# Opening of a two-layer encoder: raw x in its own tiles, two small loads on another queue, and fourteen matmuls on zeros

## The chip, the cores and the metric

One core of a Trainium2 chip runs the whole program; the other cores are idle. The metric is the device time of one execution in microseconds (us), the median of several runs. Profiles come from the hardware profiler; times in them count from the start of the span, that is from the first instruction that the profiler saw on the core. Engines are PE (TensorE), DVE (VectorE), ACT (ScalarE), POOL (GpSimd) and SP, which here only issues transfers; SPq and ACTq are the sequencers of SP and ACT, which issue them.

## What is computed

The reference is a residual trunk of two layers over 256 tokens of width 2048, in float32, with a final norm:

```python
def reference(x, norm_g, final_g, w_in_even, w_out_even, rpb_b, w_in_odd, w_out_odd, sinks_c, qnorm_d, knorm_d):
    h = x
    for layer in range(DEPTH):                     # DEPTH = 2
        y = rms_norm(h, norm_g[layer])
        if layer % 2 == 0:
            h = h + even_layer(y, w_in_even[0], w_out_even[0], rpb_b[0])
        else:
            h = h + odd_layer(y, w_in_odd[0], w_out_odd[0], sinks_c[0], qnorm_d[0], knorm_d[0])
    return rms_norm(h, final_g)
```

Each layer projects y with one wide matrix, runs two kinds of attention on the parts of the result, multiplies each by a gate and projects back. Only the first projection of the even layer matters here: `y @ w_in_even` for the first 512 columns of values ("v"), a product of 256 tokens by 2048 by 512.

## The kernel before, in words

The kernel works in float32 accuracy with a faster matmul type: each operand is cut into a high part (`hi`, rounded to that type) and a low part (`lo`, the rest), and a product is three matmuls, hi by hi, hi by lo, lo by hi (`mm3`, L100). The norm's per-token factor is applied after the projection, so the projection starts from raw x, scaled only by the norm's gain per feature (`gcol`).

Weights stream through. `plan` (L76, filled at L509 to L524) lists all weight blocks in the order of use, each 128 partitions x 1024 float32 (512 KB). `weights()` (L78) keeps two blocks ahead: a `Weights` object (L52) takes a raw buffer (`wraw`, pool `wp` with **five** buffers), loads it on SP's queue, makes `hi` on ACT (L69) and `lo` on DVE (L70), each with three buffers. A raw buffer is free again when both have read it.

The opening is the first `by_token` (L260): eight blocks j = 0 to 7 of the values' weights, called w0 to w7 below, each with the two 128-feature slices of x that multiply it (x0 to x7, 256 KB each, held transposed in DRAM as `xt`). These eight `Weights` objects also load x into `xraw`, **a second buffer of the same pool of five** (L61 to L67), and scale and cut it: `hi` by ACT (L95), `lo` by DVE (L96), the function `split`. For j = 0 both loads are cut in two halves (w0a, x0a, w0b, x0b), so that the first matmuls can start early. All these loads are `pinned` (L85): they go out in the order of the program on SP. For each j there are 12 matmuls of 512 columns (two slices, two halves of the tokens, three products each), 96 in all. Beside them `opening` (L528) issues the loads of the first two of four parts of h (x again, by token; h0 at j = 6, h1 at j = 7); the other two follow after the opening (L561).

After the opening come three projections `by_feature` (L241; q, k, gate), with four weight blocks each (the first is f0), and then attention beside further projections. A list of generators (`evac`, `bg`) is advanced by `step()` after each block: it holds `first_scale` (L535), which squares and sums h on ACT (L184) and makes the norm's factor, and then the evictions of the accumulators. The engines' instruction order is made by the framework from the program's order and the dependencies; only pinned instructions keep the program's order among themselves.

The tiles `mh0` to `mh7` (128 x 2 x 256 each) hold the results of the eight attentions of each layer; the first of them is written only when the first attention has ended. `pth` holds transposed probabilities of attention, and the PSUM tile `o` its output.

Of the kernel before, what the change touches and what calls it, by code (L numbers as in the profile page):

```python
# [9 lines left out]
F32 = mybir.dt.float32  # L10
F32R = mybir.dt.float32r
BF16 = mybir.dt.bfloat16
I32 = mybir.dt.int32
AF = mybir.ActivationFunctionType
ALU = mybir.AluOpType
AX = mybir.AxisListType

P = 128
D = 2048
S = 256  # L20
HD = 128
KC = D // P
KK = 2
NJ = KC // KK
# [3 lines left out]
BIG = 1e30  # L28
GRID_W = 64
AHEAD = 2  # L30
RPB_R, RPB_C = 15, 31


@with_exitstack
def encoder(ctx, tc, a, out):
    nc = tc.nc
    pool = lambda name, bufs, **kw: ctx.enter_context(tc.tile_pool(name=name, bufs=bufs, **kw))
    const = pool("const", 1)
    big = pool("big", 1)
    wp = pool("wp", 5)  # L40
    hp = pool("hp", 3)
    pp = pool("pp", 2)
    tp = pool("tp", 2)
# [5 lines left out]
    ps_o = pool("ps_o", 1, space=PS)  # L49


    class Weights:  # L52


        def __init__(self, src, hi=None, lo=None, x=None):
            raw = wp.tile([P, 1024], F32, tag="wraw", name="wraw")
            self.hi = hi or hp.tile([P, 1024], F32R, tag="whi", name="whi")
            self.lo = lo or hp.tile([P, 1024], F32R, tag="wlo", name="wlo")
            cuts = KK if x == 0 else 1
            cols = [slice(i * 1024 // cuts, (i + 1) * 1024 // cuts) for i in range(cuts)]  # L60
            xraw = [wp.tile([P, KK, S], F32, tag="wraw", name="xraw")] if x is not None else []  # L61
            for i, c in enumerate(cols):
                load = nc.sync.dma_start if x is None else pinned
                load(raw[:, c], src[:, c])
                for r in xraw:
                    k = slice(i, i + 1) if cuts > 1 else slice(0, KK)
                    pinned(r[:, k], a["xt"][x].rearrange("p (k t) -> p k t", k=KK)[:, k])  # L67
            for i, c in enumerate(cols):
                nc.scalar.copy(self.hi[:, c], raw[:, c])  # L69
                nc.vector.tensor_sub(self.lo[:, c], raw[:, c], self.hi[:, c].bitcast(F32))  # L70
                for r in xraw:
                    for m in (i,) if cuts > 1 else range(KK):
                        k = x * KK + m
                        split(xh[k], xl[k], r[:, m, :], gcol[:, k : k + 1])

    plan, ready = [], []  # L76

    def weights(ahead=AHEAD):  # L78

        while plan and len(ready) <= ahead:  # L80
            src, x = plan.pop(0)
            ready.append(Weights(src, x=x))
        return ready.pop(0)

    def pinned(dst, src):  # L85

        tc.keep_in_program_order(nc.sync.dma_start(dst, src))

    def split(hi, lo, src, scale=None):

        if scale is None:
            nc.scalar.copy(hi, src)
            nc.vector.tensor_sub(lo, src, hi.bitcast(F32))
        else:
            nc.scalar.mul(hi, src, scale)  # L95
            nc.vector.scalar_tensor_tensor(  # L96
                out=lo, in0=src, scalar=scale, in1=hi.bitcast(F32), op0=ALU.mult, op1=ALU.subtract
            )
# [10 lines left out]
    xh = [X[k // 4][:, k % 4, 0, :] for k in range(KC)]  # L109
    xl = [X[k // 4][:, k % 4, 1, :] for k in range(KC)]  # L110
    h = [big.tile([P, 2, 512], F32, tag=f"h{n}", name=f"h{n}") for n in range(NN)]

    gcol = const.tile([P, 2 * KC], F32, tag="gcol", name="gcol")
    nc.scalar.dma_start(gcol, a["norm_g"])
    warm = const.tile([P, 1], F32, tag="warm", name="warm")
    nc.vector.memset(warm, 0.0)
    nc.scalar.activation(warm, warm, AF.Exp)
# [10 lines left out]
    def load_h(n):  # L128
        x = a["x"].rearrange("(t p) d -> p t d", p=P)
        pinned(h[n], x[:, :, n * 512 : (n + 1) * 512])  # L130
# [17 lines left out]
    def rsqrt(dst, ss, n, mean):  # L148

        x = sm.tile([P, n], F32, tag="rs_x", name="rs_x")  # L150
        nc.vector.tensor_scalar(x, ss, mean, EPS, ALU.mult, ALU.add)
        y = sm.tile([P, n], I32, tag="rs_y", name="rs_y")
        nc.vector.tensor_scalar(y, x.bitcast(I32), -0.5, 1597463007.0, ALU.mult, ALU.add)
        y = y.bitcast(F32)
        for it in range(3):
            t = sm.tile([P, n], F32, tag="rs_t", name="rs_t")
            nc.vector.tensor_mul(t, y, y)
            nc.vector.scalar_tensor_tensor(t, t, -0.5, x, ALU.mult, ALU.mult)
            z = dst if it == 2 else sm.tile([P, n], F32, tag="rs_z", name="rs_z")
            nc.vector.scalar_tensor_tensor(z, t, 1.5, y, ALU.add, ALU.mult)  # L160
            y = z
# [18 lines left out]
    def square_sums(parts, n, t=None):  # L180

        for tt in range(2) if t is None else (t,):
            junk = tp.tile([P, 512], BF16, tag="junk", name="junk", bufs=1)
            nc.scalar.activation(junk, h[n][:, tt, :], AF.Square, accum_out=parts[:, tt, n : n + 1])  # L184

    def row_scale(layer, parts):

        ss = sm.tile([P, 2], F32, tag="ss", name="ss")
        nc.vector.tensor_reduce(ss, parts, AX.X, ALU.add)
        r = const.tile([P, 2], F32, tag=f"rstd{layer}", name=f"rstd{layer}")  # L190
        rsqrt(r, ss, 2, 1.0 / D)
        return r

    def spread_scale(r):

        bc = ps_at.tile([P, S], F32, tag="at", name="ps_bc")
        for tt in range(2):
            t = tp.tile([P, P], F32, tag="rb", name="rb")
            nc.vector.tensor_scalar_mul(t, ones, r[:, tt : tt + 1])
            nc.tensor.transpose(bc[:, tt * P : (tt + 1) * P], t, ident)  # L200
        rk = const.tile([P, S], F32, tag="rk", name="rk")
        rq = const.tile([P, S], F32, tag="rq", name="rq")
        nc.vector.tensor_copy(rk, bc)
        nc.vector.tensor_scalar_mul(rq, rk, -SCALE)
        rhalf = const.tile([P, S], F32, tag="rhalf", name="rhalf")
        nc.vector.tensor_scalar_mul(rhalf, rk, 0.5)
        return rk, rq, rhalf
# [151 lines left out]
    mh = [big.tile([P, 2, S], F32R, tag=f"mh{i}", name=f"mh{i}") for i in range(8)]  # L359
# [168 lines left out]
    def opening(j):  # L528
        if j == 2:
            make_identity(nc, ident)  # L530
            nc.gpsimd.memset(ones, 1.0)
        if j > 5:
            load_h(j - 6)

    def first_scale():  # L535
        yield
        yield
        for n in range(NN):
            square_sums(parts0, n)
        r = row_scale(0, parts0)  # L540
        yield
        scales[0] = r, spread_scale(r)
        yield
# [26 lines left out]
    for u in range(4):  # L570
        st = {}
        if u == 1:
            bg.append(later_consts())
        for pr, kind in even_order(u):
            if kind != "v":
                evac.append(evict_even(2 * u + pr, kind, by_feature(), st))
                continue
            if u:
                acc = by_token(512, token_acc())
            else:  # L580
                acc = [ps_at.tile([P, 512], F32, tag="at", name="ps_t") for _ in range(2)]
                by_token(512, acc, opening)
                bg.append(after_opening())
                evac.append(first_scale())
            st["v"] = values_tile()
            evac.append(evict_even(2 * u, kind, acc, st))
# [13 lines left out]
    def tail_even(order):  # L600
        for n in range(NN):
            accs = out_accs()
            project_out(order, accs)
            for t in range(2):
                add_h(n, t, accs[t])
            for c in range(2):
                tr = ps_at.tile([P, 2, S], F32, tag="at", name="ps_ht")
                for i in range(2):
                    for t in range(2):
                        nc.tensor.transpose(  # L610
                            tr[:, i, t * P : (t + 1) * P],
                            h[n][:, t, (2 * c + i) * P : (2 * c + i + 1) * P], ident,
                        )
                for i in range(2):
                    k = 4 * n + 2 * c + i
                    split(xh[k], xl[k], tr[:, i, :], gcol[:, KC + k : KC + k + 1])
            square_sums(parts1, n)
# [209 lines left out]
```

## Time and profile before

| | |
|---|---|
| median of 3 runs | 839.94 us (839.72 to 842.06) |
| the profiled execution | 839.72 us |
| its span, first to last instruction | 837.6 us |
| PE busy | 821.5 us, 98% of the span, 4472 matmuls |
| DVE, ACT, POOL busy | 67%, 53%, 2% |
| moved by DMA | 158.51 MB, mean 189 GB/s |
| opening: first matmul, first matmul of the next projection | 4.80 us, 30.58 us |

The profiled execution is the quickest of the three runs shown, 0.22 us below the median, and 2.1 us of it lie outside the span. A matmul's duration in the trace reaches into the next one's, since they are pipelined; the rate of the engine is read from the distance between starts.

### The profile page before, as it was taken

The numbers are of one execution on the slowest core, as the hardware profiler recorded it, in microseconds if no ns is written. First come the engines' busy times: TensorE is split into PE (matmuls) and PEld (weight loads), VectorE is DVE, ScalarE is ACT, GpSimd is POOL, SyncE is SP. The second block draws the span as 40 slices with busy tenths as digits, with TensorE's granted clock in tenths as the row PEclk, the third lists the DMA queues.
The fourth block names the chain that finished last, engine by engine and source line by source line (L and its number), as shares of the span: only waits on it lengthen the run. The fifth ranks groups of instructions, "written<-read, shape, count | busy, mean of one in ns | idle before, by whom it ended". The sixth has DMA issues, their size and how long they took to land.

```text
span 837.6 us, 11876 instructions
## 1 busy us (share of the span) xinstructions
PE 821.5 (98%) x4472; PEld 707.2 (84%) x4472; DVE 559.5 (67%) x873; ACT 445.1 (53%) x706; POOL 18.8 (2%) x24
## 2 busy tenths in 40 slices
PE   7999999999999999999999999999999999999995
PEld 5888888888888888888888888888899888888884
DVE  5677575667757675576645787786976666766547
ACT  6755454555445554455443565556666555664433
POOL 0000000000001010010000000000000000000000
PEclk9999999999999999999999999999999999999998
DMA  7976765655566565665555555654545555655622
GB/s 253 374 228 204 236 208 170 209 176 175 178 199 194 171 199 168 201 196 160 172 184 192 176 175 180 193 184 150 165 162 191 182 179 188 194 191 193 226 90 100
DMA packets 55577, 158.51 MB, mean 189 GB/s; under 512 B 14112, under 2 KB 15008, under 8 KB 55456
## 3 DMA queue, kind: packets, MB, share of 16 engines
q1 hardware_dynamic: 55376, 157.74, 57.7%
q8 instruction: 35, 0.57, 0.3%
q14 instruction: 22, 0.18, 0.1%
q10 hardware_dynamic: 144, 0.02, 0.0%
HBM read 155.64 MB, written 3.05 MB: 189 GB/s over the span
## 4 chain that ended last, share of the span: by engine, by line
PE 97%; DVE 1%; DMA 1%; ACT 0%; SPq 0%; issue 0%; DVEq 0%; ACTq 0%
PE ps_f L250 33%; PE ps_f L254 16%; PE ps_t L103 13%; PE ps_t L104 13%; PE ps_t L102 13%; PE ps_pt L439 2%; PE ps_s L103 1%; PE ps_s L104 1%; PE ps_out L103 1%; PE ps_out L104 1%; PE ps_s L102 1%; PE ps_out L102 1%; DMA wraw<-in_even_t 1%; PE ps_ht L610 0%; DVE h L495 0%; PE ps_tr L352 0%
## 5 line engine op out<-in xcount | busy, mean ns | idle before, releaser
L70 DVE TENSOR_TENSOR wlo<-wraw,whi 128x1024 fp32r<-128x1024 f32 (+1 forms) x269 | 329.5, 1225 | 209.7 <-ACT whi L69 208.6
L69 ACT CAST whi<-wraw 128x1024 fp32r<-128x1024 f32 (+1 forms) x269 | 281.8, 1048 | 345.5 <-PE ps_t L104 146.9
L250 PE MATMUL ps_f<-x,whi 128*128 128x512 f32 x1184 | 374.0, 397 | 0.0
L254 PEld LDWEIGHTS ps_f<-x,wlo 128*128 128x128 f32 x1184 | 222.3, 188 | 53.0 <-DVE wlo L70 0.7
L254 PE MATMUL ps_f<-x,wlo 128*128 128x256 f32 x1184 | 233.4, 278 | 0.0
L250 PEld LDWEIGHTS ps_f<-x,whi 128*128 128x128 f32 x1184 | 180.9, 189 | 0.4
L102 PE MATMUL ps_t<-whi,x 128*128 128x512 f32 (+1 forms) x256 | 97.7, 382 | 5.6 <-ACT x L95 5.6
L103 PE MATMUL ps_t<-wlo,x 128*128 128x512 f32 (+1 forms) x256 | 97.2, 380 | 0.3 <-DVE wlo L70 0.3
L104 PE MATMUL ps_t<-whi,x 128*128 128x512 f32 (+1 forms) x256 | 97.2, 380 | 0.0
L102 PE MATMUL ps_t<-whi,mh 128*128 128x512 f32 x240 | 94.1, 392 | 0.0
L103 PE MATMUL ps_t<-wlo,mh 128*128 128x512 f32 x240 | 94.0, 391 | 0.0
L104 PE MATMUL ps_t<-whi,ml 128*128 128x512 f32 x240 | 93.6, 390 | 0.0
L102 PEld LDWEIGHTS ps_t<-whi,x 128*128 128x128 f32 x256 | 48.4, 189 | 14.9 <-ACT x L95 6.8
L104 PEld LDWEIGHTS ps_t<-whi,x 128*128 128x128 f32 x256 | 48.4, 189 | 9.7 <-DVE x L96 0.6
L103 PEld LDWEIGHTS ps_t<-wlo,x 128*128 128x128 f32 x256 | 48.5, 189 | 9.2 <-DVE wlo L70 1.0
L104 PEld LDWEIGHTS ps_t<-whi,ml 128*128 128x128 f32 x240 | 45.1, 188 | 9.2
L103 PEld LDWEIGHTS ps_t<-wlo,mh 128*128 128x128 f32 x240 | 45.2, 188 | 8.9
L102 PEld LDWEIGHTS ps_t<-whi,mh 128*128 128x128 f32 x240 | 45.1, 188 | 8.9
L469 DVE TENSOR_TENSOR mx<-ps_out,silu 128x512 f32<-128x512 f32 x16 | 11.1, 691 | 30.1 <-PE ps_out L104 30.1
L495 DVE TENSOR_TENSOR h<-ps_t,h 128x512 f32<-128x512 f32 x32 | 21.1, 685 | 9.7 <-PE ps_t L104 9.5
L421 ACT ACTIVATE pr<-lg,mn 128x256 f32<-128x256 f32 (+1 forms) x48 | 23.9, 500 | 5.0 <-DVE mn L409 5.0
L294 DVE TENSOR_TENSOR qf<-ps_f,qf 128x512 f32<-128x512 f32 x37 | 25.2, 682 | 0.0
(116 smaller groups left out, 657.0 us busy)
## 6 DMA issues: line engine op xcount, KB each, us to landing
wraw<-in_even_f SPq DMA_DIRECT2D x96, 512.0 KB, 3.5
wraw<-in_odd_f SPq DMA_DIRECT2D x56, 512.0 KB, 3.4
wraw<-in_w_out_even SPq DMA_DIRECT2D x32, 512.0 KB, 3.3
wraw<-in_w_out_odd SPq DMA_DIRECT2D x32, 512.0 KB, 4.2
wraw<-in_even_t SPq DMA_DIRECT2D x31, 512.0 KB, 4.2
wraw<-in_odd_t SPq DMA_DIRECT2D x24, 512.0 KB, 3.6
h<-in_x SPq DMA_DIRECT2D x4, 512.0 KB, 8.0
bias<-in_bias_a SPq DMA_DIRECT2D x8, 256.0 KB, 5.2
```

What stands on the lines that cost most here:

```text
L69: nc.scalar.copy(self.hi[:, c], raw[:, c])
L70: nc.vector.tensor_sub(self.lo[:, c], raw[:, c], self.hi[:, c].bitcast(F32))
L102: nc.tensor.matmul(dst, lh, rh, start=first, stop=False, skip_group_check=True)
L103: nc.tensor.matmul(dst, lh, rl, start=False, stop=False, skip_group_check=True)
L104: nc.tensor.matmul(dst, ll, rh, start=False, stop=last, skip_group_check=True)
L250: nc.tensor.matmul(acc[:, f, :], w.hi[:, c], xx[k], start=k == 0, stop=False, skip_group_check=True)
L254: nc.tensor.matmul(acc[:, f, :S], w.lo[:, c], xh[k], start=False, stop=k == KC - 1, skip_group_check=True)
L294: nc.vector.tensor_add(f, acc[:, :, :S], f)
L421: nc.scalar.activation(p[:, t, :W], lg[:, t, :W], AF.Exp, bias=mn[:, t : t + 1], scale=-1.0, accum_out=den[:, t : t + 1],)
L439: nc.tensor.transpose(tr[:, c, t * P : (t + 1) * P], p[:, t, c * P : (c + 1) * P], ident)
L469: nc.vector.tensor_mul(m, o, silu)
L495: nc.vector.tensor_add(h[n][:, t, :], acc, h[n][:, t, :])
```

## The change

Five edits, all around the opening:

- Raw x no longer takes buffers of the weights' pool. Eight tiles with the names `mh0` to `mh7` hold it (`xraw[j]`), the same memory that later holds the results of attention. So the five raw buffers are for weights alone.
- The two halves of x0 are issued on ACT's queue, behind the load of `gcol` and ahead of ACT's table load; SP now begins with w0a, w0b, w1, x1, w2, x2.
- For j = 0 the high part of x is made on DVE instead of ACT, and ahead of the cut of the weights in program order.
- A tile of zeros is set on DVE (128 x 256, in the memory of `pth`), and 14 matmuls of it by itself (256 columns each) go into the PSUM tile `o`, ahead of all else on PE.
- h0 and h1 are loaded at j = 4 and j = 6 instead of 6 and 7; the squares on ACT are pinned; `first_scale` yields after h1 and h3, so it takes two steps more.

```diff
+WARM = 14
...
-            xraw = [wp.tile([P, KK, S], F32, tag="wraw", name="xraw")] if x is not None else []
-            for i, c in enumerate(cols):
+            for c in cols:
                 load = nc.sync.dma_start if x is None else pinned
                 load(raw[:, c], src[:, c])
-                for r in xraw:
-                    k = slice(i, i + 1) if cuts > 1 else slice(0, KK)
-                    pinned(r[:, k], a["xt"][x].rearrange("p (k t) -> p k t", k=KK)[:, k])
+            if x:
+                load_xraw(x, slice(0, KK), nc.sync)
             for i, c in enumerate(cols):
+                if x == 0:
+                    nc.vector.tensor_scalar_mul(xh[i], xraw[0][:, i, :], gcol[:, i : i + 1])
                 nc.scalar.copy(self.hi[:, c], raw[:, c])
                 nc.vector.tensor_sub(self.lo[:, c], raw[:, c], self.hi[:, c].bitcast(F32))
-                for r in xraw:
-                    for m in (i,) if cuts > 1 else range(KK):
-                        k = x * KK + m
-                        split(xh[k], xl[k], r[:, m, :], gcol[:, k : k + 1])
+                if x == 0:
+                    low_x(i)
+            if x:
+                for k in range(x * KK, (x + 1) * KK):
+                    split(xh[k], xl[k], xraw[x][:, k % KK, :], gcol[:, k : k + 1])
+
+    def load_xraw(j, k, engine):
+        src = a["xt"][j].rearrange("p (k t) -> p k t", k=KK)
+        tc.keep_in_program_order(engine.dma_start(xraw[j][:, k], src[:, k]))
+
+    def low_x(k):
+        nc.vector.scalar_tensor_tensor(
+            out=xl[k], in0=xraw[k // KK][:, k % KK, :], scalar=gcol[:, k : k + 1], in1=xh[k].bitcast(F32),
+            op0=ALU.mult, op1=ALU.subtract,
+        )
...
     nc.scalar.dma_start(gcol, a["norm_g"])
+    xraw = [big.tile([P, KK, S], F32, tag=f"mh{j}", name="xraw") for j in range(NJ)]
+    load_xraw(0, slice(0, 1), nc.scalar)
+    load_xraw(0, slice(1, 2), nc.scalar)
+    idle = tp.tile([P, S], F32R, tag="pth", name="idle")
+    nc.vector.memset(idle.bitcast(F32), 0.0)
+    ps_idle = ps_o.tile([P, S], F32, tag="o", name="ps_idle")
+    for _ in range(WARM):
+        nc.tensor.matmul(ps_idle, idle[:, :P], idle, start=True, stop=True, skip_group_check=True)
...
-            nc.scalar.activation(junk, h[n][:, tt, :], AF.Square, accum_out=parts[:, tt, n : n + 1])
+            tc.keep_in_program_order(
+                nc.scalar.activation(junk, h[n][:, tt, :], AF.Square, accum_out=parts[:, tt, n : n + 1])
+            )
...
-        if j > 5:
-            load_h(j - 6)
+        if j in (4, 6):
+            load_h(j // 2 - 2)
...
         for n in range(NN):
             square_sums(parts0, n)
+            if n % 2:
+                yield
```

## Rows read from the trace of the kernel before

**Rows 1.** Profile page, part 4: the chain that ended last, by engine

```profile
PE 97%; DVE 1%; DMA 1%; ACT 0%; SPq 0%; issue 0%; DVEq 0%; ACTq 0%
```

**Rows 2.** Chain of waits in order of time, 0 to 13 us: start, duration, what

```profile
2.57 6.18 DMA wraw<-in_even_t
...
8.78 1.06 ACT whi L69
...
9.86 1.24 DVE wlo L70
...
11.14 0.50 PE ps_t L103
```

**Rows 3.** Timeline of PE: start, duration, line, out<-in, size, count [idle before]

```profile
4.80 0.80 PE L102 MATMUL ps_t<-whi,x 128*128 128x512 f32 x1 [4.80 <-ACT x L95]
...
6.68 0.63 PE L103 MATMUL ps_t<-wlo,x 128*128 128x512 f32 x1
7.10 0.63 PE L104 MATMUL ps_t<-whi,x 128*128 128x512 f32 x1
...
10.28 0.51 PE L102 MATMUL ps_t<-whi,x 128*128 128x512 f32 x1 [0.51 <-ACT x L95]
...
19.49 0.39 PE L103 MATMUL ps_t<-wlo,x 128*128 128x512 f32 x1
...
20.11 0.40 PE L102 MATMUL ps_t<-whi,x 128*128 128x512 f32 x1
...
27.87 0.41 PE L103 MATMUL ps_t<-wlo,x 128*128 128x512 f32 x1
...
28.52 0.39 PE L102 MATMUL ps_t<-whi,x 128*128 128x512 f32 x1
...
30.58 0.61 PE L250 MATMUL ps_f<-x,whi 128*128 128x512 f32 x2
...
31.57 0.63 PE L250 MATMUL ps_f<-x,whi 128*128 128x512 f32 x2
```

**Rows 4.** Timeline of SP: the issues of w0b, w1, x2, h0 and f0

```profile
1.62 0.43 SPq L87 DMA_DIRECT2D wraw<-in_even_t  x1
...
2.57 0.43 SPq L87 DMA_DIRECT2D wraw<-in_even_t  x1
...
7.05 0.33 SPq L87 DMA_DIRECT2D xraw<-in_xt  x1
...
21.66 0.43 SPq L87 DMA_DIRECT2D h<-in_x  x1
22.18 0.42 SPq L64 DMA_DIRECT2D wraw<-in_even_f  x1
```

**Rows 5.** Windows of the opening: busy time by engine, clock, DMA share, GB/s

```profile
1.00:4.00 3.00, 0.00 (x0) 0.00 (x0) 0.00 (x0) 1.76 (x3) 0.36 (x2) 1.00 0.67 198
4.00:6.00 2.00, 1.20 (x3) 1.04 (x4) 1.09 (x2) 1.07 (x3) 0.00 (x0) 1.00 0.50 158
6.00:9.00 3.00, 2.67 (x9) 1.50 (x8) 1.17 (x2) 1.03 (x3) 0.00 (x0) 1.00 0.99 376
```

**Rows 6.** Timeline of ACT, 0 to 8 us

```profile
1.15 1.28 ACT L117 ACT_TABLE_LOAD   x1 [1.15 <-PEq L817]
...
3.72 0.62 ACT L69 CAST whi<-wraw 128x512 fp32r<-128x512 f32 x1 [1.08 <-DMA wraw<-in_even_t]
...
7.50 0.51 ACT L95 ACTIVATE x<-xraw,gcol 128x256 fp32r<-128x256 f32 x1 [1.21 <-DMA xraw<-in_xt]
```

**Rows 7.** Timeline of DVE: first release of a projection's accumulator, and a scaling

```profile
43.23 0.68 DVE L294 TENSOR_TENSOR qf<-ps_f,qf 128x512 f32<-128x512 f32 x1
...
46.34 0.28 DVE L204 TENSOR_SCALAR rq<-rk 128x256 f32<-128x256 f32 x1
```

**Rows 8.** Windows after the last matmul (columns as in Rows 5)

```profile
826.00:828.00 2.00, 1.56 (x7) 0.94 (x6) 1.89 (x8) 1.37 (x5) 0.00 (x0) 1.00 0.00 0
...
830.00:832.00 2.00, 0.00 (x0) 0.00 (x0) 1.77 (x7) 0.10 (x1) 0.00 (x0) 0.59 0.78 289
```

## The prediction, on record before the changed kernel was built

> **What bounds the kernel now.** I read the chain that ended last first: 97% of it is PE [rows 1]. From the middle of the opening to the end PE is one unbroken stream, so nothing that speeds another engine there matters; what the change can give is only the time by which this stream starts earlier. The second view, the chain in order of time [rows 2], shows what starts it: the load of w1, issued at 2.57, lands at 8.75; ACT makes its high part from 8.78, DVE its low part from 9.86 to 11.10, and at 11.14 PE goes on and hardly stops again. The third view, PE's timeline [rows 3], shows what lies before and behind this point. The first matmul is at 4.80. Early ones are 0.42 us apart (6.68 to 7.10), which is 512 columns at 1.2 GHz; later ones 0.228 us (34 steps from 20.11 to 27.87), which is 2.4 GHz. At 11.14 only 13 of 96 matmuls have run. The other 83 would take 83 x 0.228 = 18.92 us and end at 30.06; they end at 30.58. So 0.52 us are lost behind 11.14: two steps from 19.49 take 0.62 instead of 0.46, and two from 27.87 take 0.65. Four matmuls from 30.58 (two of 512 columns, two of 256, so 3 x 0.228 = 0.68) take 0.99: 0.31 lost. Together 0.83 us.
>
> Last, the transfers. SP has issued w1 by 3.0 [rows 4], but x2 goes out only at 7.05: it waits for a buffer of the five. The windows [rows 5] show that the transfer engines are not full: 594 KB by 4.0 (3 us at 198 GB/s), then a share of 0.50 and 158 GB/s from 4 to 6 although w1 is queued, then 0.99 and 376 GB/s.
>
> **The change part by part.** The reference is the profiled execution: 839.72 us, 0.22 under the median.
>
> *Zeros on PE.* Fourteen matmuls of 256 columns. No row shows one at half clock; by columns each is half of 0.42, so 14 x 0.21 = 2.9 us. They start when DVE has set the tile, about 1.2 (a set of this size should not exceed the 0.28 us of a scaling of 128 x 256 [rows 7], from about 0.8), and end at 4.2, before the first real matmul can run. Bounds: 14 x 0.114 = 1.6 us at full clock, and 14 x 0.42 = 5.9 us if each costs as much as one of 512 columns, which ends at 7.1. I take 2.9, as the cost goes by columns at 2.4 GHz too. Their use is the clock: before, the spacing shows the rise between 7.10 and 8.1, some 3.2 us after the first matmul. Started at 1.2, PE should have 2.4 GHz at about 4.4 to 5. That spares the 12 matmuls of j = 0 six times 0.2 us = 1.2 us. But this stretch lies ahead of the wait for w1: the next matmul is at 10.28 after idling [rows 3]. So I put it at nothing. The Trainium skill, in "TensorE: Matmul & The Clock Gate", section on the HAM clock gate, says that half rate is the default which activity lifts, and advises to warm up; by that page the sum would gain the 1.2 us, and by the rows none, for what PE saves there it waits.
>
> *First matmul.* DVE makes the high part of x0a beside ACT's cast, not behind it. ACT casts w0a from 3.72 [rows 6]; a scaling costs 0.28 on DVE [rows 7]. The first matmul moves from 4.80 to about 4.45. This too ends in the wait for w1: nothing. ACT issues two loads more before its table load at 1.15: two issues of 0.43 [rows 4] put the table's end from 2.43 to about 3.4, still ahead of 3.72; without that cover it delays w0a, not w1.
>
> *Order of the loads, the term that decides.* On SP, w1 goes out behind w0a and w0b alone, 1.62 instead of 2.57 [rows 4]: 0.95 earlier. The x0 halves come by ACT's queue at the same time. How much earlier does w1 land? Lower bound: nothing, if the 1311 KB up to the end of w1 pass in the same order at the same pace. Upper bound: engines full from 4.0. Then 1311 - 594 = 717 KB at 376 GB/s end at 5.9; before, that much had moved by about 7.2 (4.0 to 6.0 brought 316 KB, the other 401 KB took 1.1 us or more), while the landing came at 8.75, 1.55 us behind, as the slowest of the engines counts. 5.9 + 1.55 = 7.45, a gain of 1.3. I take 0.95, the earlier issue passed on in full, since the share of 0.50 says that transfer engines lacked work while w1 had long been issued; it is nearer to the upper bound for that reason. The wait chain behind is unchanged: landing 7.8, high part 7.83 to 8.9, low part to 10.15, stream from 10.2. The 12 matmuls of j = 0 must be done by 9.3, when w1's first x is cut: from 4.45 they need 2.7, and x0b, which landed at 7.5 [rows 6], is issued half a microsecond sooner. They are.
>
> *Buffers for weights alone.* w3 and w4 no longer wait for a buffer; x2 (before at 7.05) and what follows are issued by 5. All that PE uses after w1 lands well ahead of it. I take 0.65 of the 0.83 us of later stalls as gone, with bounds of nothing (if ACT's and DVE's own order is what is late) and 0.83.
>
> *h loads and squares.* h0 stands ahead of w6 now instead of ahead of f0 [rows 4], one load of 512 KB, 1.4 us at 376 GB/s, with several us of lead by then: nothing; without that lead, up to 1.4 us. SP waits longest for a raw buffer of w5 onward, and behind that wait stand x5 and h0, all with lead. The eight squares remain on ACT, one pair of steps later. What depends on them is the norm's factor; q's accumulator is released by a DVE addition at 43.23 that does not use it [rows 7], and the third projection needs that bank at 30.58 + 2 x (32 x 0.228 + 32 x 0.114) = 52.5. Two steps of 2.7 us later fit in: nothing; without the cover PE would stand up to 3 us there.
>
> **Sum.** 0.95 + 0.65 = 1.6 us: 839.72 - 1.6 = 838.1 for an execution like the profiled one, 838.3 as a median.
>
> **Rivals.**
>
> (a) *The supply does not move.* The two queues feed the same 16 transfer engines, w1 still lands at 8.75, and only the later stalls go: 839.94 - 0.65 = 839.3. For it: from 6 to 9 the share is 0.99, and the slowest engine decides. Against it: the half-empty stretch at 4 to 6. The Trainium skill, "DMA: Bandwidth & Descriptors", section "Issuing engines are not separate DMA queues", says that loads started from several engines interleave on the same engines and save only the issuer's time; the 0.50 of the trace says there was room, and which of them holds decides between (a) and the forecast.
>
> (b) *The supply moves more.* The hole at 4 to 6 closes and the spread between the transfer engines shrinks, so that w1 lands at 6.5 or before: 2.25 + 0.65 = 2.9 us, 837.0. The limit is a stream from 4.45: opening over at 4.45 + 96 x 0.228 = 26.3, a gain of 4.2 + 0.3 = 4.5, or 835.4. For it: no other work keeps PE then. Against it: even with full transfer engines, the sum above comes to 7.45.
>
> (c) *Slower.* PE, now early, is done with j = 0 at 7.4 and then idles until w1. If w1 lands as late as before, that is until 10.28, 2.9 us. At the end of the run the clock shows what idling does: last of seven matmuls over at 827.6, mean clock 0.59 in 830 to 832, so it fell at 830.4, 2.8 us after [rows 8]. From an idle time of that length the clock falls, and the stream begins at half rate: over the 3.2 us until it rises, 1.6 us are lost. 839.94 - 0.65 + 1.6 = 840.9. Against it: it wants a late w1 and a quick j = 0 together.
>
> **How the numbers follow.** Forecast 0.50, (a) 0.24, (b) 0.18, (c) 0.08. About 0.3%, 2.5 us, is what a measurement of this kernel can tell from no change. Faster by that needs 837.4 or less: (b), 0.18. Slower needs 842.5, which (c) reaches only together with a late release of q's bank: 0.04. Same: 0.78. The range reaches from inside (b), 836.5, to between (a) and (c), 840.3; the forecast's own bounds are 837.8 to 839.9.
>
> **What would show it.** Right: first matmul near 4.45, spacing 0.228 from about 5 on, w1's cast at about 7.8, unbroken matmuls from about 10.2, no steps of 0.3 us around the fourth and seventh block, first matmul of q near 29. Wrong: a cast of w1 at 8.7 as now, real matmuls behind zeros, spacing of 0.42 after 9 us, or a stop of PE ahead of the third projection.

## The result and the profile after

The changed kernel is a little slower: 841.38 us median of 20 runs (840.15 to 842.55) beside 839.62 for the kernel before in the same runs, ratio 1.0022 with a 95% interval of 1.0016 to 1.0028. That is 1.8 us, within the 0.3% that was taken as no change; but the interval is clear of 1, and the time lies outside the range on record (836.5 to 840.3) and on the other side of the forecast (838.3). The profiled execution took 841.35 us, with a span of 839.2; the engines' busy shares are those of before.

Three starts in PE's timeline, read in both profiles, show where the time came in. The first matmul of q is at 32.09 instead of 30.58 [rows 3], 1.51 us later. The first output of attention starts at 88.31 instead of 86.71, 1.60 later, and the last one at 763.60 instead of 761.97, 1.63 later. So the net loss arises in the opening, and nothing changes behind the first attention. Between q and the first attention two things largely cancel: a new stop of 0.53 us, shown below, and the 0.31 us at q's start [rows 3], which the changed kernel no longer loses. First output of attention, before and after:

```profile
86.71 0.28 PE L102 MATMUL ps_out<-pth,vh 128*128 128x256 f32 x1
...
88.31 0.28 PE L114 MATMUL ps_out<-pth,vh 128*128 128x256 f32 x1
```

The chain in order of time, 0 to 14 us, of the changed kernel (the view of [rows 2]):

```profile
0.71 0.41 ACTq L126
...
1.15 0.46 ACTq L80
...
1.64 6.12 DMA xraw<-in_xt
...
7.78 0.04 DVE x L69
...
8.05 0.70 DVE wlo L71
...
8.79 0.80 PE ps_t L115
9.59 0.43 PE ps_t L116
```

The load of w1 no longer stands in the chain. What stands there is the second half of x0, on ACT's queue behind the gains (`gcol`), whose issue starts at 1.64 and which lands at 7.76; then a scaling of it on DVE, and only then a low part of the weights, with which PE goes on at 8.79. Why the low part comes behind the scaling is seen in DVE's timeline, 0 to 11 us:

```profile
5.12 0.35 DVE L69 TENSOR_SCALAR x<-xraw,gcol 128x256 fp32r<-128x256 f32 x1 [4.00 <-DMA xraw<-in_xt]
5.51 0.48 DVE L83 SCALAR_TENSOR_TENSOR x<-xraw,gcol,x 128x256 fp32r<-128x256 f32 x1
7.78 0.35 DVE L69 TENSOR_SCALAR x<-xraw,gcol 128x256 fp32r<-128x256 f32 x1 [1.79 <-DMA xraw<-in_xt]
8.05 1.29 DVE L71 TENSOR_TENSOR wlo<-wraw,whi 128x512 fp32r<-128x512 f32 x2
```

The high part of x0b (7.78) stands in DVE's instruction order **ahead of** the low part of w0a (the first of the two at 8.05). ACT had cast w0a at 3.69 and w0b at 4.85, so both low parts could have been made from 5.5 on; DVE, which takes its instructions in order, stood 1.79 us for x0b instead. The framework fixes that order, and none of these six instructions is pinned.

PE's timeline of the same stretch:

```profile
1.17 3.35 PE L134 MATMUL ps_idle<-idle 128*128 128x256 f32 x14 [1.17 <-DVE warm L136]
5.62 1.19 PE L114 MATMUL ps_t<-whi,x 128*128 128x512 f32 x2 [1.10 <-DVE x L69]
8.79 0.80 PE L115 MATMUL ps_t<-wlo,x 128*128 128x512 f32 x1 [1.98 <-DVE wlo L71]
9.38 0.63 PE L116 MATMUL ps_t<-whi,x 128*128 128x512 f32 x1
9.81 0.63 PE L115 MATMUL ps_t<-wlo,x 128*128 128x512 f32 x1
...
12.79 0.40 PE L116 MATMUL ps_t<-whi,x 128*128 128x512 f32 x1
13.02 0.62 PE L114 MATMUL ps_t<-whi,x 128*128 128x512 f32 x2
...
32.09 0.62 PE L272 MATMUL ps_f<-x,whi 128*128 128x512 f32 x2
```

The zeros run from 1.17 to about 4.5. Two real matmuls follow at 5.62; they need no low part. Then PE waits until 8.79. From there it never waits in the opening again, but the first ten matmuls take 4.23 us (8.79 to 13.02), 0.43 us each once the stream runs: 1.2 GHz, the lower level. The other 84 take 0.227 us each: 8.79 + 4.23 + 84 x 0.227 = 32.09, so no other stop is left. At 0.227 us ten take 2.27, so about 1.95 us are lost.

These levels are read from the distance between starts. The clock column of the windows reads 1.00 all through the opening, in [rows 5] too, because the trace holds no record of the granted clock before its first rise, and the column counts that stretch as full. The first record starts at 7.76 in the kernel before and at 12.76 in the changed one, which agrees with the spacing; such starts are called clock records below.

The windows (columns as in [rows 5]) show that the transfers did what the forecast wanted:

```profile
4.00:6.00 2.00, 0.90 (x4) 0.63 (x4) 0.84 (x2) 0.93 (x2) 0.00 (x0) 1.00 0.99 363
6.00:9.00 3.00, 1.02 (x3) 0.30 (x3) 1.22 (x3) 1.42 (x3) 0.00 (x0) 1.00 1.05 419
```

The half-empty stretch is full (share 0.99 for 0.50), and ACT casts w1 as soon as it lands:

```profile
7.58 1.05 ACT L70 CAST whi<-wraw 128x1024 fp32r<-128x1024 f32 x1 [2.11 <-DMA wraw<-in_even_t]
```

7.58 instead of 8.78. The price is in x0: x0a is there at 5.1, where the kernel before had it by 4.25 at the latest, and x0b at 7.76, later than the 7.5 of [rows 6] though issued earlier.

One wait lies behind the opening, in PE's and DVE's timelines around 55 us:

```profile
55.06 0.30 PE L222 MATMUL ps_bc<-ident,rb 128*128 128x128 f32 x1 [0.53 <-DVE rb L221]
```

```profile
51.15 0.15 DVE L211 TENSOR_REDUCE ss<-parts 128x2 f32<-128x8 f32 x1
...
54.36 0.16 DVE L180 SCALAR_TENSOR_TENSOR rstd<-rs_t,rs_z 128x2 f32<-128x2 f32 x1
54.63 0.48 DVE L221 TENSOR_SCALAR rb<-ones,rstd 128x128 f32<-128x128 f32 x2
```

The norm's factor is now made from 51.15 to 54.36, and PE, in whose order the two transposes that spread it stand, stops 0.53 us ahead of the first; before, they ran at 44.25 without a stop.

### The profile page after: what moved, and what is told of

Read it like the earlier page. It is cut to its first block, busy times and chain, and to the rows that moved or that the text cites. A ratio compares the mean times of both kernels' runs of the same rounds, so it can differ in the third digit from the quotient of the medians.

```text
span 839.2 us, 11893 instructions
## 1 busy us (share of the span) xinstructions
PE 824.4 (98%) x4486; PEld 711.6 (85%) x4486; DVE 560.3 (67%) x876; ACT 443.6 (53%) x704; POOL 18.4 (2%) x24
## 4 chain that ended last, share of the span: by engine, by line
PE 96%; DVE 2%; DMA 1%; ACT 1%; issue 0%; ACTq 0%; DVEq 0%
PE ps_f L272 32%; PE ps_f L276 16%; PE ps_t L115 13%; PE ps_t L116 13%; PE ps_t L114 13%; PE ps_pt L461 2%; PE ps_s L116 1%; PE ps_s L115 1%; PE ps_out L115 1%; PE ps_out L116 1%; PE ps_s L114 1%; PE ps_out L114 1%; DMA xraw<-in_xt 1%; PE ps_ht L634 0%; DVE wlo L71 0%
## 5 line engine op out<-in xcount | busy, mean ns | idle before, releaser
L491 DVE TENSOR_TENSOR mx<-ps_out,silu 128x512 f32<-128x512 f32 x16 | 11.1, 691 | 29.8 <-PE ps_out L116 29.8
```

The source lines that it names most:

```text
L491: nc.vector.tensor_mul(m, o, silu)
```

## The experiments

Two theories at first. **A**: the order on DVE holds PE until x0b is there, and then the clock is low; a smaller part is the wait at the norm's factor. **B**: what costs is the late landing of x0 by ACT's queue, whatever DVE does. Each run was timed beside the kernel before on the same chip, which was at 839.35 to 839.57.

### 1. DVE's order pinned

```diff
+                keep = tc.keep_in_program_order if x == 0 else lambda ins: ins
                 if x == 0:
-                    nc.vector.tensor_scalar_mul(xh[i], xraw[0][:, i, :], gcol[:, i : i + 1])
+                    keep(nc.vector.tensor_scalar_mul(xh[i], xraw[0][:, i, :], gcol[:, i : i + 1]))
                 nc.scalar.copy(self.hi[:, c], raw[:, c])
-                nc.vector.tensor_sub(self.lo[:, c], raw[:, c], self.hi[:, c].bitcast(F32))
+                keep(nc.vector.tensor_sub(self.lo[:, c], raw[:, c], self.hi[:, c].bitcast(F32)))
...
-        nc.vector.scalar_tensor_tensor(
+        tc.keep_in_program_order(nc.vector.scalar_tensor_tensor(
```

> The changed kernel with DVE's six instructions of j = 0 pinned in program order, so that the low part of w0a no longer stands behind the scaling of x0b. Theory A (DVE's order holds PE): the first matmul with a low part moves from 8.79 to about 6.2, PE runs from 5.6 without the stop of 2 us, the first nine or ten real matmuls are at half clock, q's projection starts at 29.7 (+-0.5) instead of 32.09, and the time falls by 2.4 us to about 839.0. Rival B (the late landing of x0 by ACT's queue holds PE, 5.1 and 7.75): PE stands again until x0b is there, q starts at 31 or later, and the time stays at 841 or above.

Measured: 838.6 us (838.27 to 839.33), ratio to before 0.9991 (0.9981 to 1.0). PE's timeline:

```profile
5.62 1.19 PE L115 MATMUL ps_t<-whi,x 128*128 128x512 f32 x2 [1.09 <-ACT whi L71]
6.61 1.05 PE L116 MATMUL ps_t<-wlo,x 128*128 128x512 f32 x2
7.46 1.05 PE L117 MATMUL ps_t<-whi,x 128*128 128x512 f32 x2
8.50 1.19 PE L115 MATMUL ps_t<-whi,x 128*128 128x512 f32 x2
...
29.99 0.62 PE L273 MATMUL ps_f<-x,whi 128*128 128x512 f32 x2
```

The stop of 2 us is gone, the low part runs at 6.61, q starts at 29.99, and the kernel is 2.8 us quicker than the changed one by the medians, 2.6 by the two ratios, with x0b landing no earlier than there (DVE scales it at 8.00). So B falls as the main cause: at the lower clock the late x0b by itself holds PE for some 0.2 us here (two matmuls from 7.46 would be through at 8.31, the next starts at 8.50). It cost more because the low parts stood behind it. At the higher clock PE is ready sooner and does stop for it (run 7).

### 2. No zeros, and 3. forty zeros

> The changed kernel without the zeros, their tile and the 14 matmuls. Theory A: the zeros raised nothing, the clock rises at about 13.0 as with them, the time is the same within 0.3 us (841.4). Rival C (the zeros do lift the clock in most executions, the profiled one was unlucky): slower by up to 2 us. Rival D (the zeros are in the way of something): faster by 0.5 us or more.

> The changed kernel with 40 zero matmuls instead of 14, so that PE is busy from 1.2 until about 7 to 9.7. Theory A (what is lost beside DVE's order is the clock, which fell short because PE stopped at 4.4): 2.4 GHz is granted before 8.8, the stream from 8.8 runs at 0.228 us from its first matmul, q starts at about 30.2, the time falls by 1.9 us to about 839.5. Rival E (matmuls on zeros don't lift the clock at all): the clock rises only 3 to 4 us after the real stream begins, zeros end at 9.7, q starts at 33 and the time rises by 0.9 us to 842.3.

Run 2 takes the tile of zeros and its matmuls out; run 3 has `WARM = 40`. Without zeros: 841.46 us (840.62 to 842.79), the same as with 14, and the matmul spacing falls to 0.23 us only at 13.1. With forty: 839.67 us (838.89 to 839.92), 1.7 us quicker than the changed kernel. Its PE timeline:

```profile
1.17 6.29 PE L134 MATMUL ps_idle<-idle 128*128 128x256 f32 x40 [1.17 <-DVE warm L136]
7.29 0.39 PE L114 MATMUL ps_t<-whi,x 128*128 128x512 f32 x1
8.92 0.50 PE L115 MATMUL ps_t<-wlo,x 128*128 128x512 f32 x1 [1.23 <-DVE wlo L71]
9.26 0.40 PE L116 MATMUL ps_t<-whi,x 128*128 128x512 f32 x1
9.50 0.40 PE L114 MATMUL ps_t<-whi,x 128*128 128x512 f32 x1
...
30.63 0.62 PE L272 MATMUL ps_f<-x,whi 128*128 128x512 f32 x2
```

Forty matmuls of zeros take 6.1 us (1.17 to 7.29), which is 0.153 each on average, between 0.21 at the lower clock and 0.114 at the higher: the clock rose on zeros alone (clock record 4.00). PE still waits for the low part (8.92), but the stream behind it runs at 0.23 from the start. The 14 of the change ended 1.1 us ahead of the first real matmul and 4.3 us ahead of the stream, and brought nothing there (run 2). Runs 1 and 3 mend the two halves of the same loss and don't add: 2.8, 1.7 and the 0.55 of run 4 would make 5.05, and run 7, with 24 zeros, has 3.15 from all three.

### 4. Loads of h, squares and steps as before

```diff
-            tc.keep_in_program_order(
-                nc.scalar.activation(junk, h[n][:, tt, :], AF.Square, accum_out=parts[:, tt, n : n + 1])
-            )
+            nc.scalar.activation(junk, h[n][:, tt, :], AF.Square, accum_out=parts[:, tt, n : n + 1])
...
-        if j in (4, 6):
-            load_h(j // 2 - 2)
+        if j > 5:
+            load_h(j - 6)
...
-            if n % 2:
-                yield
```

> The changed kernel with the loads of h, the squares and the steps of first_scale as before. Theory A: the stop of 0.53 us at the spreading of the norm's factor (55.06) goes and q starts as in the changed kernel (32.1): 0.4 us less, 841.0. Rival F (the earlier h loads are what delays the opening): q starts earlier by 0.5 us or more, 840.4 or less.

Measured: 840.83 us (840.03 to 841.81), 0.55 less than the changed kernel; q starts at 32.08, as there. PE's list of waits has no entry for the norm's factor any more:

```profile
PE ps_t L115 <- DVE wlo L71: 2.2, 1, 2.2
PE ps_idle L134 <- DVE warm L136: 1.2, 1, 1.2
PE ps_t L114 <- DVE x L69: 1.0, 1, 1.0
```

So this edit cost about half a microsecond behind the opening and gave nothing in it.

### 5. x0 on SP, and 6. the tiles alone

Run 5 issues the halves of x0 on SP between those of w0, as before, and keeps the rest of the change:

```diff
-    load_xraw(0, slice(0, 1), nc.scalar)
-    load_xraw(0, slice(1, 2), nc.scalar)
...
-            for c in cols:
+            for i, c in enumerate(cols):
                 load = nc.sync.dma_start if x is None else pinned
                 load(raw[:, c], src[:, c])
+                if x == 0:
+                    load_xraw(0, slice(i, i + 1), nc.sync)
```

Run 6 goes the other way, the kernel before with one edit:

```diff
+    xtile = [big.tile([P, KK, S], F32, tag=f"mh{j}", name="xraw") for j in range(NJ)]
...
-            xraw = [wp.tile([P, KK, S], F32, tag="wraw", name="xraw")] if x is not None else []
+            xraw = [xtile[x]] if x is not None else []
```

> The changed kernel with the two halves of x0 issued on SP between w0a, w0b and w1, as before, instead of on ACT; the framework then puts the low part of w0a ahead of the scaling of x0b on DVE by itself. Theory A: x0a lands at 4.1, PE starts at 4.6 and has no stop of 2 us ahead of a low part of w0a; w1 lands at 8.7 as before, since five transfers are ahead of its issue again, so the stream begins at 11.1; q starts at 29.9 (+-0.4), the time is 839.2. Rival G (it was the buffers, not the queue, that brought w1 forward): w1 lands at 7.6, the stream begins at 10, q starts at 28.9, 838.2. Rival B (the order on DVE is not the cause): no better than the changed kernel, 841.

> The kernel before with one edit: raw x in the tiles of the attention results, so that the weights have all five raw buffers; all loads stay on SP in the old order, no zeros, high parts on ACT. Theory A: w1 lands at 8.7 as before, the stream begins at 11.1, only the later stops (0.83 us in all) go: q starts at 29.9, 838.8. Rival G (buffers bring w1 forward): w1 lands near 7.6, the stream begins at 10, q starts at 28.9, 837.9. Rival H (the buffers were never short): nothing changes, q at 30.6.

Run 5: 838.9 us (837.98 to 840.75), ratio 0.9994 (0.9986 to 1.0003); x0a is scaled at 4.16, ACT casts w1 at 8.46, q starts at 29.55. Its edit moves only the loads of x0, and its transfers leave the hole at 4 to 6 us half open (columns as in [rows 5]):

```profile
4.00:6.00 2.00, 1.86 (x9) 1.19 (x8) 1.35 (x3) 0.98 (x2) 0.00 (x0) 1.00 0.79 213
```

Run 6: 838.05 us (837.64 to 838.75), ratio 0.9985 (0.9976 to 0.9994); ACT casts w1 at

```profile
8.83 1.04 ACT L69 CAST whi<-wraw 128x1024 fp32r<-128x1024 f32 x1 [1.55 <-DMA wraw<-in_even_t]
```

and the windows show the hole of the kernel before, little filled:

```profile
4.00:6.00 2.00, 1.17 (x3) 1.01 (x4) 1.09 (x2) 0.78 (x2) 0.00 (x0) 1.00 0.66 200
6.00:9.00 3.00, 3.00 (x9) 2.21 (x8) 1.12 (x2) 1.29 (x3) 0.00 (x0) 1.00 0.97 323
```

So G falls: buffers alone don't bring w1 forward, moving x0 to the second queue does, by which w1 is also issued earlier on SP (w1 is cast at 7.3 to 8.2 in the runs with x0 on ACT, 8.5 to 8.8 in those without). Whether the earlier place on SP alone would do it, with x0 issued behind w1 there, was not tried. But the buffers alone make the kernel 1.3 us quicker than before:

```profile
30.17 0.61 PE L251 MATMUL ps_f<-x,whi 128*128 128x512 f32 x2
```

q starts 0.41 us earlier, the 0.31 us that were lost at its start are saved too, and the first output of attention is 1.03 us earlier (85.68). Theory A had 0.83 for this; the interval, 0.5 to 2.0 us, holds that.

### 7. Pinned order, 24 zeros, h as before

> The changed kernel with three edits together: DVE's order of j = 0 pinned, 24 zero matmuls instead of 14, the loads of h and the squares as before. Theory A (three separate losses that add): 2.4 GHz is granted before or soon after the first real matmul (5.6), j = 0 ends at about 9.3 behind x0b, the stream of j = 1 goes on at 10.4 with 13 or 14 matmuls done, q starts at 29.1, no stop at the norm's factor: 837.3. Rival (the clock falls again in the wait for x0b between 7 and 8.4, or rises late): q at 29.9, 838.1.

Measured: 838.23 us (836.89 to 838.6), ratio 0.9983 (0.9974 to 0.9992). q starts at 29.85, not at 29.1: the rival's number, but not its mechanism, for the spacing is at 0.23 from 7.1 on. PE stopped for x0b, and then for low parts one after the other: DVE scaled x0b at 8.19, made the low part of w0b at 8.46, x0b's low part at 9.06 and w1's from 9.46 to 10.68. The edit had left one low part (w0b) behind the scaling of x0b.

### 8. The pinned order without zeros

> The changed kernel with DVE's order of j = 0 pinned and without the zeros. Theory A (14 zeros that end at 4.4 bring no clock): rise some 3 to 5 us after the first real matmul at 5.4, q starts at 30.0 (+-0.3), the time is as with the 14 zeros and the pinned order, 838.6 (+-0.3). Rival C (the zeros do help there): rise a microsecond or more later than the 10.86 seen with them, 839.2 or more.

Measured: 839.6 us (838.68 to 841.51), ratio 1.0006 (0.9996 to 1.0015); with the 14 zeros, on another chip, it was 838.6, and the intervals of the two ratios touch. By the median, rival C holds. The profiles don't show it: the clock records are 10.28 without zeros and 10.62 with them, and q starts at 30.15 and 29.99. One execution of each is profiled, and the rise differs between executions (below); what 14 zeros are worth on average there is not settled.

### 9. Both low parts of w0 ahead of x0b

The kernel of run 7, with the scaling of x0b moved behind the low part of w0b on DVE:

```diff
-                if x == 0:
-                    keep(nc.vector.tensor_scalar_mul(xh[i], xraw[0][:, i, :], gcol[:, i : i + 1]))
+                high_x = lambda: keep(nc.vector.tensor_scalar_mul(xh[i], xraw[0][:, i, :], gcol[:, i : i + 1]))
+                if x == 0 and i == 0:
+                    high_x()
                 nc.scalar.copy(self.hi[:, c], raw[:, c])
                 keep(nc.vector.tensor_sub(self.lo[:, c], raw[:, c], self.hi[:, c].bitcast(F32)))
+                if x == 0 and i == 1:
+                    high_x()
```

> The kernel with pinned order, 24 zeros and h as before, and on DVE the low part of w0b as well moved ahead of the scaling of x0b. Theory A (what waits on DVE behind x0b's landing at 8.2 still sets the stream): low parts of w1 end 0.6 us earlier, at about 10.1, q starts at 29.2 instead of 29.85, the time is 837.6, 0.6 below the kernel without this edit (838.2). Rival (w1's landing near 8.0 and ACT's cast set it): less than 0.2 us.

Measured: 837.79 us (836.85 to 838.15), ratio 0.9982 (0.9973 to 0.999): by the median the quickest of the study, and quicker than both kernels. DVE's and PE's timelines:

```profile
6.15 0.69 DVE L73 TENSOR_TENSOR wlo<-wraw,whi 128x512 fp32r<-128x512 f32 x1
7.81 0.35 DVE L69 TENSOR_SCALAR x<-xraw,gcol 128x256 fp32r<-128x256 f32 x1 [0.98 <-DMA xraw<-in_xt]
8.20 0.49 DVE L87 SCALAR_TENSOR_TENSOR x<-xraw,gcol,x 128x256 fp32r<-128x256 f32 x1
8.71 1.23 DVE L73 TENSOR_TENSOR wlo<-wraw,whi 128x1024 fp32r<-128x1024 f32 x1
```

```profile
1.17 5.49 PE L138 MATMUL ps_idle<-idle 128*128 128x256 f32 x24 [1.17 <-DVE warm L140]
6.46 0.60 PE L118 MATMUL ps_t<-whi,x 128*128 128x512 f32 x1
6.88 0.40 PE L119 MATMUL ps_t<-wlo,x 128*128 128x512 f32 x1
7.12 0.40 PE L120 MATMUL ps_t<-whi,x 128*128 128x512 f32 x1
...
8.31 0.47 PE L118 MATMUL ps_t<-whi,x 128*128 128x512 f32 x1
...
29.09 0.62 PE L274 MATMUL ps_f<-x,whi 128*128 128x512 f32 x2
```

w1's low part starts at 8.71 (9.46 in run 7), and q at 29.09 (29.85), as expected. The medians of the two runs differ by 0.44 us, less than their intervals can tell apart; so do those of this run and run 6, the tiles alone, by 0.26.

### 10. Zeros on the tiles alone, 11. x0 on SP with all repairs, 12. run 9 without zeros

> The kernel before with raw x in its own tiles, as in the run of the tiles alone, and 24 zero matmuls ahead. Theory A (before w1 the matmuls of j = 0 have time to spare, so the clock is worth nothing there): 2.4 GHz by 8 us at the latest, but the stream still begins at 11.1 behind w1, q at 30.0 (+-0.2), the time as with the tiles alone, 838.05 (+-0.3). Rival I (the clock matters beyond j = 0): 0.5 us or more faster. Rival J (after a longer wait for w1 the clock falls again): slower by 1 us or more.

> The kernel with pinned order, x0 on SP, 20 zeros, h as before. Theory A: w1 lands at 8.4 to 8.8, the stream begins at 10.8 to 11.1, no stop at the norm's factor: q at 29.6, 838.3, that is 0.5 below the run with x0 on SP alone. Rival (pinned order or h cost something here): 838.9 or more.

> The quickest kernel so far (pinned order, both low parts of w0 ahead of the scaling of x0b, h as before, 24 zeros) without its zeros. Theory A (where DVE no longer stops PE, the clock sets the pace of the first stream, and enough zeros are worth a microsecond): the first real matmul moves to 5.2, but 2.4 GHz comes only at 8.5 to 10.5, the second half of j = 0 runs at half rate, q starts at 29.8 to 30.3 instead of 29.09, the time is 838.7 (+-0.4) instead of 837.8. Rival K (w1's landing leaves PE time to spare, the zeros are worth nothing): q at 29.1, 837.8.

Run 10: 838.45 us (837.13 to 839.95), ratio 0.9992 (0.9984 to 1.0001); the clock record is 5.97, j = 0 is done early, PE then waits for w1 and q starts at 29.92. No better than the tiles alone: ahead of a wait the clock is worth nothing that these runs can tell, as the prediction had it for the kernel before. Run 11: 838.27 us (837.65 to 839.01), ratio 0.9987 (0.9978 to 0.9996), q at 29.59, both as in theory A. Run 12: 838.29 us (837.52 to 840.52), ratio 0.9986 (0.9977 to 0.9995); the spacing falls to 0.23 only at 11.1, q starts at 29.99, 0.9 later than with 24 zeros. Its median is 0.5 above run 9's, not clear by the intervals; the profiles point to A.

## Why the prediction was wrong

**The step that failed** is the sentence that "the 12 matmuls of j = 0 must be done by 9.3", with "They are" behind it. They were counted from 4.45 with a need of 2.7 us, by what PE, ACT and the landings allow, and at 0.228 us each, the higher clock. DVE's queue was not looked at, though the change puts two instructions into it, the scalings of x0a and x0b, and each waits for a transfer. An instruction that waits for a load holds all that stands behind it on its engine; behind x0b's scaling stood the low parts of w0a and w0b, for which a third of j = 0's matmuls wait directly and nearly all others in PE's order. In the end two matmuls of j = 0 had run at 8.79 instead of twelve (run 1: with the order mended, 2.8 us less). Even then the twelve were not done by 9.3: in run 1, mostly at 0.43 us each and from 5.62 on, they took until 10.94.

**What came true of the sum.** w1 by 0.95 earlier: its cast moved from 8.78 to 7.58, 1.2 us; the hole at 4 to 6 did mean transfer engines without work, and it is the move to the second queue, not the buffers, that closed it (363 GB/s, beside 213 in run 5 and 200 in run 6). The later stops, 0.65: they are gone in the changed kernel (spacing 0.227 from 13.02 to 32.09), and alone were worth more than that by the median, 1.3 us with an interval that reaches down to 0.5 (run 6). Zeros: 14 took 0.21 to 0.24 us each and ended by 4.5, near the 4.2 that was priced.

**The first matmul** was put at 4.45, from x0a's old landing. It came at 5.62, since x0a by ACT's queue landed at 5.1. The last of w0, x0 and w1 was there at 7.76 (x0b) instead of 8.75 (w1), 0.99 earlier for 0.95 of issue time saved on SP. The Trainium skill, in "DMA: Bandwidth & Descriptors", section "Issuing engines are not separate DMA queues", says that issuing on several engines saves only the issuer's time; the trace agrees in size. Within these loads the order changed: w1 landed 1.2 earlier, and x0a, issued at the same 1.15, at least 0.85 later. It went behind `gcol` on the second queue; whether that is why was not tried.

**The clock** was given up as worth nothing, "for what PE saves there it waits". That holds where PE waits behind it (run 10). Here the wait came before the stream, so the stream began at the lower clock and paid about 1.95 us. Run 3, where it began at the higher one, was 1.7 us quicker. Rival (c), at 0.08, had this mechanism, a stop and then half rate, at 1.6 us; its cause for the stop, a late w1, was another, and in the profile the clock had not risen before the stop.

**The norm's factor** was put at nothing, by looking at who waits for the accumulator. The one that waits is PE itself, in whose order the two transposes stand: 0.53 us in the profile, 0.55 in run 4.

## What to carry to other kernels

When an instruction is moved to another engine, list what stands behind it in that engine's order and what it waits for; an instruction that waits for a late load belongs behind those whose inputs are already there, and where a framework chooses the order, that order must be read, and pinned where it matters, not assumed. Warm-up matmuls paid where they reached up to the real ones (run 3, 1.7 us); ahead of a wait for a load 24 of them gave nothing that could be measured (run 10), nor did 14 that ended 1.1 us ahead of the first real one (run 2). Of the five edits, the one that only ended a shortage of buffers gained by itself, 1.3 us; it needed none of the others, and no run with more of them is clearly quicker.

## What the runs showed of the hardware that was not expected

- Matmuls on zeros do lift the clock (run 3). From the first matmul of such a block to the clock record it took 2.8 us (run 3), 4.8 (run 10), 5.7 (runs 7 and 9) and 6.1 (run 11); in the last three real matmuls had begun by then. After 14 of them, 3.3 us long, the clock record is 10.6 to 12.8 in three profiles (the changed kernel, runs 1 and 4), and 4.51 in run 5, after the same 14 at the same times and ahead of the first real matmul (4.66). What decides between these was not tried.
- Two small loads moved to the second queue landed later themselves, and yet the transfers as a whole ran at 363 GB/s where the kernel before had moved 158 in the same two microseconds [rows 5], and run 5, whose edit takes back this move alone, 213.
